# Gate and up of a SwiGLU feed-forward by seven products of block sums instead of eight, in three token blocks, with the last attention head reordered and merged in two halves

## The chip, the cores and the metric

One Trainium2 chip; the kernel runs on one core of it. Its engines are TensorE (PE in the profile; PEld is its weight load), VectorE (DVE), ScalarE (ACT), GpSimd (POOL) and SyncE (SP, which here issues the DMAs). The metric is the device time of one launch in microseconds; a kernel's time is the median of several runs.

## The reference

One layer for a prompt of 2048 tokens and a sample group of 8 x 4 tokens, all in float32, D = 1024, FF = 2816:

```python
z = rmsnorm(x, norm1_g) @ w_in                     # -> q, k, v (8 heads of 64), u, vg (8 groups of 64)
att = merge(three dilated sliding-window branches) # weights: each branch's share of the softmax sums
gate = spatial_gate(layernorm(vg)) 
x = x + concat([att, u * gate]) @ w_out
h = rmsnorm(x, norm2_g)
x = x + (silu(h @ w_gate) * (h @ w_up)) @ w_down
y = rmsnorm(x, final_g)
```

It returns y of both groups, the last keys and values of both, and the normalised v rows of the sample.

## The kernel before

Every operand of a matmul is a pair of float32r tiles, a high part and the low rest (`split_sb`, L120 to L126: the high part is a cast by ACT or DVE, the low part a subtraction, on POOL unless said otherwise), and every product is three matmuls: hi·hi, hi·lo, lo·hi. The engines' orders are written out by hand. In the attention part each piece of work is put at a step and a phase (`at(step, phase, fn)`), and a plan runs them in that order; in the feed-forward part `later(n, fn)` puts a piece n ticks ahead, and `tick()` runs what is due. Each engine works through its own queue in the order of issue and waits where an operand isn't ready.

The attention heads come one after another, 20 items each (16 band blocks, 4 strided groups "s"), in the order FIRST or OTHER. When a head's items are done, its softmax sums are brought into one layout (`stats_a` to `stats_c`, L959 to L974), turned into branch weights (`weights_a`, `weights_b`), written to a DRAM buffer f_d (`weights_store`) and read back in four chunks of 512 tokens (`merge_load`), by which the branches' outputs are multiplied and added (`merge`, L1008 to L1017, three steps per chunk) and stored (`merge_store`). For the last head this happens beside the start of the output projection: one chunk on DVE, three on POOL.

After that the tokens are worked through in two blocks, Block(0, 8) with 8 tiles of 128 tokens, and Block(8, 16), 8 tiles and the sample's 32 rows. In each: output projection (`out_part`, L1277 to L1279, k-tiles loaded by `load_cat`, split by `split_cat`, two halves of 512 columns), residual addition (`out_end`), RMSNorm (`norm2_a` to `norm2_c`; ACT squares, DVE multiplies by the factor and the gain, PE transposes, ACT and DVE split), then the feed-forward over 22 tiles f of 128 hidden columns:

- `load_gate` and `load_down` fetch 512 KB each for gate, up and down of one f; `split_gate` makes high and low parts of 128x1024 (ACT, POOL), `split_down` the same (DVE, POOL).
- `gate_unit` (L1336): for each slice of tokens (512 wide in block 1, 352 in block 2) 8 k-tiles for gate and 8 for up, three matmuls each (L1346 to L1348), into a PSUM tile of two banks, of which there are two; then ACT's silu (L1350), DVE's multiplication (L1351), high part on DVE (L125), low part on POOL (L126).
- `down_unit` (L1357): after each pair of f, for each token tile and each half of 512 columns, two f times three matmuls (L1372), and DVE's addition to the residual (L1374). PSUM has two banks for it.

At the end of a block come the final norm (`final_a`, `final_b`, L1377 to L1397: by DVE in one instruction, or for the first five tiles of the last block by ACT and POOL) and the store. Pieces of the caches (`roll`) are copied from DRAM to DRAM beside it.

## Time and profile before

| | |
|---|---|
| median of 3 runs | 2746.23 us (2745.55 to 2747.11) |
| the profiled execution | 2748.68 us, its span 2746.9 us |
| mean granted TensorE clock | 0.981 |
| instructions | 33610 |
| matmuls, gate and up / down | 3 x 1760 / 2112 |
| DMA | 367.44 MB, 134 GB/s over the span |

The page of the profile gives each engine's busy time with its share of the span, the granted clock and the DMA's share in slices, the chain of work that ended last (followed back from the last instruction, at each step to what released it), and the costliest groups: line, engine, operation, output<-inputs, shape, count | busy time, mean ns of one | idle time of the engine ahead of them and what ended it. The views used beside it are the groups with shapes kept apart, the busy time by stretch of the span, the chain in order of time, and the timeline (start, length, engine, line, operation, shape, count, in brackets the idle time before and its releaser).

### The profile page before, as it was taken

Reading aid. Unit: us, or ns where it says so; the run is one execution under the profiler, and the core shown is the slowest. Engines: PE = TensorE matmul, PEld = TensorE weight load, DVE = VectorE, ACT = ScalarE, POOL = GpSimd, SP = SyncE. Lnnn points to the kernel's source line nnn. Section 1 sums busy time; section 2 is a strip of 40 time slices with the busy share of each in tenths; the row PEclk is TensorE's granted clock in tenths of the full one; section 3 lists DMA queues with packets and bytes.
Section 4 is the critical chain, followed back from the end, with each engine's and each line's share of the span. In section 5 each row is a group of like instructions: output and inputs, shape, how many; then the busy total and the mean of one; then the engine's idle time right before and its main releaser. Section 6 shows DMA issues by size and latency. Waiting matters only on the chain.

```text
span 2746.9 us, 33610 instructions
## 1 busy us (share of the span) xinstructions
PE 2637.4 (96%) x13058; PEld 2234.2 (81%) x13058; DVE 1190.0 (43%) x2274; ACT 772.9 (28%) x1456; POOL 853.4 (31%) x561
## 2 busy tenths in 40 slices
PE   8998899998999989999999999999999999999997
PEld 6776777778888868888888888878899999999996
DVE  3268784436888755222222222264333232233225
ACT  6423344446777733100000001032200000000003
POOL 1035743231544542322222222211232222222222
PEclk9999999998999999999999999999999999999999
DMA  8664844685667473322222222272132222222211
GB/s 247 215 199 150 279 140 139 197 269 177 206 189 231 120 214 105 133 92 92 92 92 92 92 92 92 84 235 93 67 121 92 86 83 82 86 78 92 92 47 64
DMA packets 285476, 367.44 MB, mean 134 GB/s; under 512 B 18535, under 2 KB 214296, under 8 KB 279300
## 3 DMA queue, kind: packets, MB, share of 16 engines
q1 hardware_dynamic: 270948, 342.61, 38.2%
q10 hardware_dynamic: 14368, 22.68, 3.2%
q8 instruction: 103, 1.69, 0.3%
q14 instruction: 57, 0.47, 0.1%
HBM read 309.88 MB, written 125.47 MB: 158 GB/s over the span
## 4 chain that ended last, share of the span: by engine, by line
PE 61%; DVE 2%; DMA 1%; ACT 1%; SPq 0%; issue 0%; POOL 0%; ACTq 0%; DVEq 0%
PE ps_o L1372 18%; PE ps_s L1346 12%; PE ps_s L1347 12%; PE ps_s L1348 12%; PE ps_o L1279 2%; PE ps_o L1277 2%; PE ps_o L1278 2%; PE ps_t L1330 1%; DVE s L132 0%; DVE acc L1396 0%; DMA xl<-cat_d 0%; DMA acc<-in_x_prompt_dram 0%; DMA raw<-f_d 0%; DVE acc L1374 0%; SPq L1260 0%
## 5 line engine op out<-in xcount | busy, mean ns | idle before, releaser
L1346 PE MATMUL ps_s<-xh,gh 128*128 128x352 f32 (+1 forms) x1760 | 624.8, 355 | 0.0
L1348 PE MATMUL ps_s<-xh,gl 128*128 128x352 f32 (+1 forms) x1760 | 621.2, 353 | 0.0
L1347 PE MATMUL ps_s<-xl,gh 128*128 128x352 f32 (+1 forms) x1760 | 620.4, 352 | 0.0
L1372 PE MATMUL ps_o<-dw,hw 128*128 128x512 f32 x2112 | 500.0, 397 | 8.5 <-DVE acc L1374 8.5
L1372 PEld LDWEIGHTS ps_o<-dw,hw 128*128 128x128 f32 x2112 | 396.6, 189 | 107.0 <-DVE acc L1374 14.1
L1350 ACT ACTIVATE zn<-ps_s 128x352 f32<-128x352 f32 (+1 forms) x110 | 57.0, 518 | 1319.1 <-PE ps_s L1348 1319.1
L1351 DVE TENSOR_TENSOR zn<-zn,ps_s 128x352 f32<-128x352 f32 (+1 forms) x110 | 64.7, 588 | 722.8 <-ACT zn L1350 722.8
L1346 PEld LDWEIGHTS ps_s<-xh,gh 128*128 128x128 f32 x1760 | 332.6, 189 | 33.2
L1347 PEld LDWEIGHTS ps_s<-xl,gh 128*128 128x128 f32 x1760 | 331.8, 189 | 31.3
L1348 PEld LDWEIGHTS ps_s<-xh,gl 128*128 128x128 f32 x1760 | 330.8, 188 | 32.0
L1374 DVE TENSOR_TENSOR acc<-acc,ps_o 128x512 f32<-128x512 f32 x352 | 241.1, 687 | 214.5 <-PE ps_o L1372 214.5
L126 POOL TENSOR_TENSOR hw<-zn,hw 128x512 fp32r<-128x512 f32 (+2 forms) x110 | 119.6, 1087 | 662.4 <-DVE hw L125 648.8
L126 POOL TENSOR_TENSOR gl<-fr,gh 128x1024 fp32r<-128x1024 f32 x88 | 211.6, 2426 | 130.4 <-ACT gh L123 130.4
L126 POOL TENSOR_TENSOR dw<-fr,dw 128x1024 fp32r<-128x1024 f32 x44 | 106.6, 2422 | 377.6 <-DVE dw L125 377.6
L304 PE MATMUL ps_s<-wh,xh 128*128 128x512 f32 x480 | 198.9, 414 | 5.6 <-ACT xh L123 5.6
L305 PE MATMUL ps_s<-wl,xh 128*128 128x512 f32 x480 | 192.0, 400 | 1.2 <-DVE wl L212 1.2
L306 PE MATMUL ps_s<-wh,xl 128*128 128x512 f32 x480 | 191.8, 400 | 0.0
L304 PEld LDWEIGHTS ps_s<-wh,xh 128*128 128x128 f32 x480 | 93.3, 194 | 35.3 <-issue 8.4
L306 PEld LDWEIGHTS ps_s<-wh,xl 128*128 128x128 f32 x480 | 92.7, 193 | 20.8 <-DVE xl L126 0.2
L305 PEld LDWEIGHTS ps_s<-wl,xh 128*128 128x128 f32 x480 | 93.6, 195 | 19.3 <-DVE wl L212 2.1
L851 DVE CUSTOM_DVE_ANT_0 e<-ps_s,b 128x640 f32<-128x640 f32 (+4 forms) x128 | 93.7, 732 | 8.1 <-PE ps_s L845 8.1
L856 ACT ACTIVATE e<-e,st 128x640 f32<-128x640 f32 (+4 forms) x128 | 96.2, 751 | 0.8 <-DVE st L851 0.5
(368 smaller groups left out, 4012.2 us busy)
## 6 DMA issues: line engine op xcount, KB each, us to landing
out_ks_dram<-in_cache_k_dram SPq DMA_DIRECT2D x56, 512.0 KB
out_vs_dram<-in_cache_v_dram SPq DMA_DIRECT2D x56, 512.0 KB
fr<-in_w_gate_dram SPq DMA_DIRECT2D x44, 512.0 KB
fr<-in_w_up_dram SPq DMA_DIRECT2D x44, 512.0 KB
fr<-in_w_down_dram SPq DMA_DIRECT2D x44, 512.0 KB
raw<-in_w_in_dram SPq DMA_DIRECT2D x72, 256.0 KB
qk_d<-pair SPq DMA_DIRECT2D x64, 256.0 KB
pair<-f_d ACTq DMA_DIRECT2D x26, 512.0 KB
```

Of the source, the lines that this page charges most:

```text
L126: (eng_lo or pool).tensor_sub(lo, src, hi.bitcast(F32))
L304: pe.matmul(o[j], xh[:, k, :], wh, start=(k == 0), stop=False)
L305: pe.matmul(o[j], xh[:, k, :], wl, start=False, stop=False)
L306: pe.matmul(o[j], xl[:, k, :], wh, start=False, stop=(k == KD - 1))
L851: dve.tensor_tensor_reduce(e[:, 0:w], s[:, c0:c0 + w], d["b12"][:, 640 - w:640], 1.0, BIG, OP.add, OP.min, st[:, 0, n:n + 1])
L856: act.activation(e[:, 0:w], e[:, 0:w], AF.Exp, bias=st[:, 0, n:n + 1], scale=-1.0, accum_out=st[:, 1, n:n + 1])
L1346: pe.matmul(ps[:, q_, 0:n], wh[:, ks], B.xh[:, k, a:b], start=(k == 0), stop=False)
L1347: pe.matmul(ps[:, q_, 0:n], wh[:, ks], B.xl[:, k, a:b], start=False, stop=False)
L1348: pe.matmul(ps[:, q_, 0:n], wl[:, ks], B.xh[:, k, a:b], start=False, stop=(k == KD - 1))
L1351: dve.tensor_mul(sg[:, 0:n], sg[:, 0:n], ps[:, 1, 0:n])
L1372: pe.matmul(ps[0:nr], l_, r_[:, cs], start=(z == 0 and y == 0), stop=(z == FC - 1 and y == len(ops) - 1))
L1374: dve.tensor_add(B.acc[i][0:nr, cs], B.acc[i][0:nr, cs], ps[0:nr])
```

## The change

**Gate and up.** For a tile of 128 tokens and one f the two products gate and up are one product of a 2x2 block matrix (tokens in halves of 64; the 1024 inputs in halves of 512; columns gate and up). Winograd's form of Strassen's scheme computes it from seven block products instead of eight, with sums of blocks on both sides. The seven token operands are made once in a block, in `norm2_c`; the four sums of weight blocks and the seven splits for each f (`sums_a`, `sums_b`, `operand`); `product` runs the seven products of an f and combines them on the way. Each product has 4 k-tiles x 3 matmuls, 64 columns for each tile of the block (and 4 sample columns for each tile of the last block).

**Blocks.** Three: tiles 0 to 5, 6 to 11, and 12 to 15 with the sample; a matmul is 384, 384 and 272 columns wide. f = 0 runs in two units (tiles 0 to 3 and 4, 5; in the last block two and two). The downs of a pair of f run inside the next even f, after products 2 to 5; those of the last pair at the start of the next block. Weights are fetched once for each block.

**Engines.** In `norm2_b` and `final_b` ACT multiplies by the factor and POOL by the gain, where DVE did both (in `final_b` for all tiles of the first two blocks). The high part of the down weights comes from ACT, the low part from POOL for an even f and from DVE for an odd one. The low part of the operands of products 3 and 6 of the next f comes from DVE where f is even, all others from POOL.

**Last head.** Its items come in the order LAST; its first half of rows is brought to weights inside the head (steps 14 to 16), chunks 0 and 1 are merged there, one on DVE and one on POOL, and stored; chunks 2 and 3 follow in `first_block`. Of the head before it, the last chunk and store come later. `Stats` holds the functions of before with a range of rows.

```diff
+    class Stats:
+        def __init__(self, h, st, r0=0, r1=P):
...
+        def store(self):
+            n = self.r1 - self.r0
+            act.dma_start(dap(f_d, self.h * 2 * T + self.r0 * NT, [[NT, n], [T, 2], [1, NT]]), self.f[self.r0:self.r1, 0:2, :])
...
+    LAST = [0, "s", 1, "s", 2, "s", 3, "s", 4, 5, 6, 7] + list(range(8, NT))
...
+            stats_of(h, [(x + y, ph) for y, ph in ((14, "early"), (14, "turn"), (15, "early"), (15, "misc"), (16, "early"), (16, "mid"))], 0, 64)
+            at(x + 18, "mid", merge_load, h, 0)
+            at(x + 18, "mid", merge_load, h, 1)
+            for part in range(3):
+                at(x + 20 + part, "store", merge, h, 0, dve, part)
+                at(x + 20 + part, "store", merge, h, 1, pool, part)
+            at(x + 23, "store", merge_store, h, 0, 2)
...
+    TOK = (0, 4, 1, 3, 5, 2, 6)
...
     def fraw():
-        return pool_["fw"].tile([P, 1024], F32, name="fr", tag="fr", bufs=2)
+        return pool_["fw"].tile([P, 512], F32, name="fr", tag="fr", bufs=6)
+    def op_tile():
+        t_ = pool_["fg"].tile([P, 2, 512], F32R, name="op", tag="op", bufs=8)
+        return t_[:, 0], t_[:, 1]
...
     def norm2_b(B, i, xn, s1):
-        dve.scalar_tensor_tensor(xn[:n], B.acc[i][:n], r, gain[0][:n], op0=OP.mult, op1=OP.mult)
+        act.activation(xn[:n], B.acc[i][:n], AF.Copy, scale=r)
+        pool.tensor_mul(xn[:n], xn[:n], gain[0][:n])
...
+        def sums_of():
+            act.activation(t4, b12, AF.Copy)
+            dve.tensor_sub(t1, t4, b11)
+            dve.tensor_sub(t3, b22, t4)
+            dve.tensor_sub(t2, b22, t1)
+            dve.tensor_sub(t4, b21, t2)
...
+            for s_, j in zip(sums, (3, 5)):
+                split_sb(at_(hi, j, j + 2), at_(lo_, j, j + 2), s_)
...
+    def sums_a(f):
+        a11, a21, a22, a12 = (ab.pop((f, q)) for q in range(4))
+        s3, s2 = (raw_tile(), raw_tile()) if f == 0 else (lambda t_: (t_[:, 0], t_[:, 1]))(pair_tile(F32))
+        dve.tensor_sub(s3, a11, a21)
+        dve.tensor_add(a21, a21, a22)
+        dve.tensor_sub(s2, a21, a11)
+        ab[f] = [a11, s2, a12, a21, s3, s2, a22]
+    def sums_b(f):
+        dve.tensor_sub(ab[f][5], ab[f][2], ab[f][1])
+    def operand(f, q, eng_lo=None):
+        ops[f, q] = op_tile()
+        split_sb(*ops[f, q], ab[f][q], eng_lo=eng_lo)
...
+    def split_down(f, eng_lo=None):
+        wd[f % FC] = ob_pair("dw")
+        split_sb(*wd[f % FC], raws.pop(("d", f)), eng_lo=eng_lo)
+    def product(B, u, q):
...
+        if q % 2 == 0:
+            u["s"] = ps_s() if q < 6 else ps_t()
...
+        for k in range(4):
+            ks = slice(k * P, (k + 1) * P)
+            pe.matmul(out, wh[:, ks], xh[:, :, k], start=(k == 0), stop=False)
+            pe.matmul(out, wh[:, ks], xl[:, :, k], start=False, stop=False)
+            pe.matmul(out, wl[:, ks], xh[:, :, k], start=False, stop=(k == 3))
...
+        if q == 0:
+            act.activation(c11, ps, AF.Copy)
+        elif q == 1:
+            dve.tensor_add(c12, c11, ps)
+        elif q == 2:
+            dve.tensor_add(c11, c11, ps)
+            act.activation(c11, c11, AF.Silu)
+        elif q == 3:
+            act.activation(c22, ps, AF.Copy)
+        elif q == 4:
+            dve.tensor_add(c21, c12, ps)
+            pool.tensor_add(c12, c12, c22)
+            pool.tensor_add(c22, c22, c21)
+        elif q == 5:
+            dve.tensor_add(c12, c12, ps)
+            act.activation(c12, c12, AF.Silu)
+        elif q == 6:
+            dve.tensor_add(c21, c21, ps)
+            dve.tensor_mul(c12, c12, c22)
+            dve.tensor_mul(c11, c11, c21)
...
+                split_sb(hi, lo_, g[:, :, 0:64], eng_hi=dve)
...
-        if i < B.nt - 3 and B.last:
+        if i < B.nt - 3 or not B.last:
             act.activation(x, x, AF.Copy, scale=r)
             pool.tensor_mul(x, x, gain[1][:n])
...
-    blocks = [Block(0, 8), Block(8, NT)]
+    blocks = [Block(0, 6), Block(6, 12), Block(12, NT)]
...
+            if f + 1 < NF:
+                if q == 0:
+                    sums_a(f + 1)
+                operand(f + 1, q, dve if f % 2 == 0 and q in (3, 6) else None)
+                if q == 3:
+                    sums_b(f + 1)
+            loads_ = {0: (0, 1), 2: (2,), 4: (3,)}.get(q, ())
+            if f + 2 < NF:
+                quarters(f + 2, *loads_)
...
+            if f % 2 == 0 and q == 6:
+                split_down(f)
+                load_down(f + 1)
+            elif f % 2 == 1 and q == 3:
+                split_down(f, eng_lo=dve)
...
+            for q in range(7):
+                one(u, q)
+                if u["f"] % 2 == 0 and u["f"] > 0 and 2 <= q < 6:
+                    downs_of((B.h[0], B.h[1]), *((0, 1), (1, 2), (2, 4), (4, 9))[q - 2])
...
-    nc = _bacc.Bacc("TRN2", target_bir_lowering=False, num_devices=1)
+    nc = _bacc.Bacc("TRN2", target_bir_lowering=False, num_devices=1, dynamic_dma_scratch_size=1024)
```

The prediction names lines of the changed kernel: L1411 to L1413 are the three sums in `sums_a`, L1447 to L1449 the matmuls in `product`, L1457 the addition at q = 1 there.

More of the change, by code (lines that the diff above doesn't have):

```diff
@@ L1062, in hymba_step @@
         r4 = 0
[L1063 removed]
+        for n in FIRST if h == 0 else LAST if h == H - 1 else OTHER:
             if n == "s":
@@ new lines, in next_block @@
+    def next_block(B, downs):
+        n = len(B.rows)
+        order = [n - 1] * B.last + list(range(B.nt))
+        B.banks = (tuple(order[0:2]), tuple(order[2:4]), tuple(order[4:6]))
+        B.place()
+        tiles = [i for i in order if B.rows[i] == P]
+        for i in tiles[:2]:
+            load_cat(B, i, 0, KD)
+        skip = n - len(tiles)
+        for j, i in enumerate(tiles):
+            if j > 1:
+                later(2 * j - 1, load_cat, B, i, 0, KD)
+            later(4 + 2 * (j + skip), split_cat, B, i)
+        later(1, half1_load, 0, 1, 2, 3, 4, 5)
+        k = len(downs) + 1
+        for y, i in enumerate(order):
+            later(k + 2 * y + 5, open_end, B, i)
+        for y, what in enumerate(([(half1_split, B, 0, 1)], [(half1_split, B, 2, 3), (half1_load, 6, 7)],
+                                  [(half1_split, B, 4, 5), (quarters, 0, 0, 1)], [(half1_split, B, 6, 7), (quarters, 0, 2, 3)],
+                                  [], [(quarters, 1, 0, 1)])):
+            later(k + y, both, *what)
+        for fn in downs:
+            fn()
+        for i in order:
+            open_unit(B, i)
+        first_operands(1)
+        for i in order:
+            second_end(B, i, second_unit(B, i))
+        if B.last:
+            norm2_c(B, n - 1, B.xns)
```

570 lines of the change are left out of this document (294 added, 276 removed).

## The prediction

> **What bounds the kernel now.** I read the page first: the share of each engine, then the chain that ended last by engine, then the costliest groups.
>
> ```profile
> span 2746.9 us, 33610 instructions
> PE 2637.4 (96%) x13058; PEld 2234.2 (81%) x13058; DVE 1190.0 (43%) x2274; ACT 772.9 (28%) x1456; POOL 853.4 (31%) x561
> PE 61%; DVE 2%; DMA 1%; ACT 1%; SPq 0%; issue 0%; POOL 0%; ACTq 0%; DVEq 0%
> L1346 PE MATMUL ps_s<-xh,gh 128*128 128x352 f32 (+1 forms) x1760 | 624.8, 355 | 0.0
> L1372 PE MATMUL ps_o<-dw,hw 128*128 128x512 f32 x2112 | 500.0, 397 | 8.5 <-DVE acc L1374 8.5
> ```
>
> TensorE is busy 96% of the span, and the last chain is its own work; the gate/up products (three lines like L1346) and the downs (L1372) stand idle for 0.0 and 8.5 us. An average over stages doesn't tell where the idle rest lies, so next come the busy times by stretch: the change of stage from attention to the output projection, block 1's FFN, the change of block, block 2's projection end, block 2's FFN, the tail. Columns: stretch, its length, then PE, PEld, DVE, ACT, POOL busy with counts, granted clock, DMA share, GB/s.
>
> ```profile
> 965.00:1030.00 65.00, 52.58 (x221) 40.70 (x221) 32.89 (x49) 20.03 (x37) 25.07 (x16) 0.92 0.75 225
> 1100.00:1813.00 713.00, 713.00 (x3058) 574.18 (x3056) 181.89 (x279) 69.65 (x92) 206.27 (x106) 1.00 0.28 96
> 1813.00:1834.00 21.00, 16.82 (x62) 11.95 (x60) 18.82 (x45) 8.20 (x19) 0.00 (x0) 0.92 1.09 317
> 1936.00:1951.00 15.00, 9.97 (x58) 8.82 (x56) 11.03 (x25) 8.41 (x16) 2.82 (x1) 0.89 0.00 0
> 1951.00:2702.00 751.00, 751.00 (x4172) 698.48 (x4173) 212.56 (x355) 69.97 (x108) 215.14 (x150) 1.00 0.25 84
> 2702.00:2747.00 45.00, 26.27 (x110) 19.17 (x108) 32.55 (x71) 19.42 (x35) 13.05 (x7) 0.89 0.25 97
> ```
>
> In both FFN stretches PE is busy all the time at clock 1.00: there a matmul removed is time removed, until another engine becomes late. POOL works 206.3 + 215.1 = 421 us there, DVE 394. The idle of the four other stretches is 12.4 + 4.2 + 5.0 + 18.7 = 40.3 us.
>
> **What the change takes from TensorE.** Busy times of matmuls overlap, so the price of one is the distance between starts. I take 512 wide from one step of the chain of waits, the others from the timeline.
>
> ```profile
> 1133.09 22.39 PE ps_o L1372 x96
> 2088.12 0.32 PE L1348 MATMUL ps_s<-xh,gl 128*128 128x352 f32 x1
> ...
> 2094.95 0.33 PE L1348 MATMUL ps_s<-xh,gl 128*128 128x352 f32 x1
> 916.29 0.34 PE L896 MATMUL ps_o<-ph,ve 128*128 128x384 f32 x1
> 916.47 0.33 PE L896 MATMUL ps_o<-pl,ve 128*128 128x384 f32 x1
> 916.64 0.28 PE L896 MATMUL ps_o<-ph,ve 128*128 128x256 f32 x1
> 916.76 0.28 PE L896 MATMUL ps_o<-pl,ve 128*128 128x256 f32 x1
> 907.57 0.27 PE L945 MATMUL ps_o<-el,v 128*128 128x128 f32 x1
> ...
> 908.24 0.28 PE L945 MATMUL ps_o<-el,v 128*128 128x128 f32 x1
> ```
>
> 512 wide: 22.39 / 96 = .233 us. 352: the two quoted starts are 42 matmuls apart, 6.83 / 42 = .163. 384: .17 to .18; 256: .12; 128: 6 steps, .67 / 6 = .112. The line through 512 and 352 (.44 ns a column) puts 384 at .176, which fits, and 272, which no row shows, at .127. From below it is bounded by the 256 row (.12), from above by the 352 row (.163); I take .127, next to the 256 row.
>
> Before, the 22 gate/up tiles f cost 22 × 48 × 2 = 2112 matmuls of 512 in block 1 and 22 × 48 × 3 = 3168 of 352 in block 2: 492.5 + 515.1 = 1007.6 us. After, each f has 7 products × 4 k-tiles × 3 = 84 matmuls, 384 wide in blocks 1 and 2, 272 wide in block 3, and f = 0 runs as two units. Blocks 1 and 2: 21 × 84 × .176 + 84 × .12 (256) + 84 × .112 (128) = 330 each; block 3: 1764 × .1273 + 168 × .112 = 243.4. Sum 903.4: **104 us less**. Downs, transposes and output projection keep their number.
>
> **What it adds beside TensorE.** Per f seven operands of 128x512 are made where two of 128x1024 were, after four sums of weights on DVE; the weights are read for three blocks instead of two; the combining of products is two ACT copies, five DVE additions and two POOL additions on top of what was there. The prices:
>
> ```profile
> L126 POOL TENSOR_TENSOR dw<-fr,dw 128x1024 fp32r<-128x1024 f32 x22 | 52.7, 2395 | 201.0 <-DVE dw L125 201.0
> L126 POOL TENSOR_TENSOR hw<-zn,hw 128x352 fp32r<-128x352 f32 x44 | 41.5, 942 | 191.0 <-DVE hw L125 191.0
> L1351 DVE TENSOR_TENSOR zn<-zn,ps_s 128x352 f32<-128x352 f32 x65 | 33.8, 521 | 354.8 <-ACT zn L1350 354.8
> L125 DVE CAST hw<-zn 128x320 fp32r<-128x320 f32 x21 | 6.9, 327 | 0.7
> 311.04 1.28 POOL L521 TENSOR_TENSOR pr<-kv,qb 96x512 f32<-96x512 f32 x1
> 311.31 4.05 DVE L212 SCALAR_TENSOR_TENSOR wl<-raw,g1c,wh 128x512 fp32r<-128x512 f32 x1 [2.53 <-ACT wh L206]
> ...
> 313.53 1.28 POOL L521 TENSOR_TENSOR pr<-kn,qb 128x512 f32<-128x512 f32 x1
> 996.86 1.77 DVE L1268 TENSOR_TENSOR xl<-xl,xh 128x512 fp32r<-128x512 f32 x1
> 998.04 1.74 POOL L1015 TENSOR_TENSOR o<-o,zn 128x512 f32<-128x512 f32 x1
> 998.55 1.64 DVE L1268 TENSOR_TENSOR xl<-acc,xh 128x384 fp32r<-128x384 f32 x1
> 1001.69 0.68 DVE L1268 TENSOR_TENSOR xl<-xl,xh 128x512 fp32r<-128x512 f32 x1
> 1002.36 0.56 DVE L1268 TENSOR_TENSOR xl<-acc,xh 128x384 fp32r<-128x384 f32 x1
> ```
>
> POOL takes 2.40 for 128x1024, 1.28 for 128x512, and by the 352 row about 1.03 for 384. An odd f costs it seven operands (9.0), two low parts of the hidden values (2.0) and two additions (2.0): 13.0 us beside 84 × .176 = 14.8 of PE; an even f has five operands and a down (6.4 + 2.4 + 4.0 = 12.8), and PE has the downs as well. So POOL's total (about 846 us against 421) isn't a bound. But the last rows show that a DVE instruction with two SBUF sources and a POOL instruction don't run together: one 128x512 subtraction on DVE takes .68 alone and 4.05 while POOL's instructions (the first and the last of three quoted) run beside it; at 996 to 1000 us they alternate (DVE starts at 996.86 and 998.55, POOL between them at 998.04), a pair in 1.6 to 1.7, which is POOL's 1.28 and some .4 for DVE.
>
> The place where this reaches PE follows from the order of the changed program. PE's products 4 and 5 of a unit use the PSUM tile of products 0 and 1, which is free when DVE has added product 1 (L1457). On DVE's queue, ahead of that addition in an odd f, stand: the end of the f before (addition, two multiplications, two casts: .56 + .56 + .56 + .36 + .36 = 2.4), the low part of operand 6, and the three weight sums (L1411 to L1413). All four of these last have two SBUF sources, and POOL at that time has ready: two low parts of hidden values, the 2.40 of an even down, the first operand: 1.03 + 1.03 + 2.40 + 1.28 = 5.7 us. If they alternate as at 996 us, the addition is done at 2.4 + 5.7 + 4 × .4 + .3 (rest of the last sum) + .56 = 10.6 after the end of the unit before; PE is there at 4 × 12 × .176 = 8.45. **PE waits 2.1 us in each of 20 odd units of blocks 1 and 2: 42 us.** In an even f the down is off POOL (5.7 − 2.4), the subtraction is off DVE, and downs stand between PE's products: no wait. In block 3 PE is there at 4 × 12 × .127 = 6.1, DVE (narrower) at 10.2: 4.1; and the downs in the next even f, due after product 2 (4.6), find the low hidden part about 2.4 late in the same alternation: **6.5 × 10 = 65**. From below this is zero (rival 1). From above, each of the four instructions waits for everything ready on POOL, as at 311 us; POOL's 5.7 can't pass twice, so this changes the order, not the sum. I take the alternation: the row at 996 us has the same shapes.
>
> The Trainium skill ("SBUF — State Buffer", section "SBUF: two separate sides") says that a GpSimd instruction, or a DVE one with two SBUF inputs, takes the shared port pair for its whole length and blocks the other. The blocking agrees with the 4.05; the length does not quite, since whole lengths would make a pair 1.28 + .68 = 1.96, and the rows show 1.6 to 1.7. By the page each of the four would cost .68 rather than .4, 1.1 us more in 30 units, and the result would be some 33 us higher.
>
> **Transitions.** There are now two changes of block and three ends of projection. The chain to the first product goes through ACT and POOL for the gain and seven token operands per tile. The final norm's POOL multiplication now serves all tiles of blocks 1 and 2; in the tail that gives:
>
> ```profile
> 2725.42 3.07 PE L1372 MATMUL ps_o<-dw,hw 128*128 128x512 f32 x12 [0.21 <-DVE acc L1374]
> 2726.03 2.40 POOL L1394 TENSOR_TENSOR acc<-acc,final_g 128x1024 f32<-128x1024 f32 x1 [1.72 <-ACT acc L1393]
> ...
> 2726.27 2.18 DVE L132 SCALAR_TENSOR_TENSOR s<-s 128x1 f32<-128x1 f32 x1
> ...
> 2729.55 3.06 PE L1372 MATMUL ps_o<-dw,hw 128*128 128x512 f32 x12 [1.06 <-DVE acc L1374]
> 985.03 7.51 DMA raw<-f_d
> 985.97 0.80 PE L1277 MATMUL ps_s<-gh,xh 128*128 128x512 f32 x1 [4.75 <-ACT xh L1267]
> ...
> 992.04 0.60 PE L1278 MATMUL ps_s<-gl,xh 128*128 128x512 f32 x1
> 992.47 0.40 PE L1279 MATMUL ps_s<-gh,xl 128*128 128x512 f32 x1
> ```
>
> A tile's period is 4.13 instead of 12 × .233 = 2.8 us: the norm's 128x1 step on DVE lasts as long as POOL's multiplication beside it, and the additions that free PSUM stand behind it. For two block changes I take 5 each (the row of the one: 4.2), for three projection ends 6 each (one now: 5.0, longer chain), for the start 10 (now 12.4, half of the merge is gone from it), for the tail 15 (now 18.7; the block is half as long): 53 against 40.3, **+13**. Bounds: no change, and double the increase (0 to +26).
>
> The last head's order and half merge: the load of f_d took 7.51 us, and the merge of chunks 0 and 1 now follows it inside the head, where DVE may wait some 2.5 us in its order and PE, with work of other items queued, may not. 0, bounds −4 and +4. The weights' third reading: DMA share was .28 and .25 in the FFN; per f the same bytes come in three quarters of the time, at most .4. No cost; if a quarter came late, PE would wait at product 0.
>
> **The sum.** 2748.7 (profiled execution: span 2746.9 and 1.8 around it) − 104 + 42 + 65 + 13 + 0 = 2764.7. The median of the runs, 2746.23, is 2.5 lower: **2762**.
>
> **Rivals.**
> *Rival 1: the alternation doesn't reach PE, faster.* Should the sums get in ahead of POOL's 2.40 (the down's high part comes from ACT, behind operand 6's, so it may be ready late), DVE is done at 10.6 − 2.4 = 8.2, ahead of PE, and only block 3 waits, about 2 × 10 = 20. 2762 − 107 + 20 = 2675; 2655 to 2700. For it: DVE is idle over half the time. Against it: the alternation at 996 us needs only that both have work.
> *Rival 2: the waits cost clock, slower still.* After 4.75 idle the quoted matmuls start .43 apart until 992.5, then .233: 14 of them lose about 3 us. If block 3's 4.1 us waits each do that, + 30: 2792; if blocks 1 and 2's waits grow to 4 as well, 2815 and more. It decides at some length of the wait up to that 4.75; against it speaks that block 3's 4.1 is shorter.
> The Trainium skill ("TensorE: Matmul & The Clock Gate", section "Part 1: The HAM clock gate") has the clock halved after a stretch without activity of a few us; the row at 985.97 agrees.
> That the change doesn't remove what it says is excluded: the changed program's order has the 84 matmuls.
>
> **How the numbers follow.** The forecast's case, 2735 to 2790, .48 (.02 of it faster, .08 within 0.2%, .38 slower); rival 1 .33; rival 2 .15; something better than all of these, below 2655, .04. 0.2% (2740.7 to 2751.7) is about what a measurement of this kernel can tell from no change. Faster .02 + .33 + .04 = .39, same .08, slower .38 + .15 = .53. The range 2668 to 2818 leaves out the lower third of rival 1, the rest below it and the top of rival 2, some .2. The slower cases' own range is 2752 to 2790.
>
> **What would show it.** Product lines with starts .176 and .127 apart; the three sums' mean well over .68 (1.3 to 1.7); in odd f a PE wait at product 4 released by the addition L1457, 2.1 us in blocks 1 and 2, 4.1 in block 3; a pair of f in 48.5 us (46.4 without waits), block 3 40.7 (34.2); POOL near 55% in the FFN; clock under 1.00 in block 3 for rival 2. If the sums' mean stays near .7 and L1457 releases nothing, step and forecast are wrong and rival 1 holds.

## The result, and the profile after

The changed kernel takes 3052.47 us (median of 4 runs, 3047.75 to 3056.89) where the kernel before takes 2745.89 in the same comparison: a ratio of 1.112 (95% interval 1.109 to 1.114). The forecast was 2762, its range ended at 2818. The profiled execution took 3056.9 us, 308 more than that of before.

The page of the changed kernel, in the lines that answer to those shown of before:

```profile
span 3055.1 us, 38250 instructions
PE 2674.5 (88%) x13578; PEld 2321.2 (76%) x13578; DVE 1768.3 (58%) x3073; ACT 1134.8 (37%) x2175; POOL 1487.6 (49%) x1138
PE 51%; DVE 15%; ACT 5%; issue 4%; POOL 4%; DMA 3%; SPq 1%; ACTq 0%; DVEq 0%; POOLq 0%
L1500 PE MATMUL ps_o<-dw,hw 128*128 128x512 f32 x2112 | 516.2, 397 | 12.1 <-DVE acc L1502 4.7
```

TensorE is busy 88% instead of 96%, and the last chain goes through DVE, ACT, POOL and the DMA for a quarter of the span, where it had been TensorE's own work. The groups by line say where TensorE stands idle; the numbers behind the last bar are the idle time and the three releasers that ended most of it.

```profile
L1447 PE MATMUL ps_s<-xh,op 128*128 128x384 f32 (+4 forms) x1656 | 574.3, 347 | 199.9 <-DVE zn L1464 88.1 <-DVE raw L1459 64.1 <-ACT raw L1455 20.1
L1365 PE MATMUL ps_t<-ident,pair 128*128 128x128 f32 x128 | 23.6, 344 | 48.2 <-POOL pair L1350 43.4 <-DVE xl L1384 4.8
```

Two hundred microseconds ahead of the products, and none of the three releasers is L1457, the addition that the forecast had named. Ahead of the norm's transposes 48 us, where before it was 5.0:

```profile
L1330 PE MATMUL ps_t<-ident,pair 128*128 128x128 f32 (+1 forms) x136 | 19.0, 281 | 5.0 <-DVE xl L1334 5.0
```

The busy times by stretch (end of the first projection, the feed-forward of blocks 1, 2 and 3) have the clock in the column after the five engines:

```profile
1083.00:1115.00 32.00, 22.47 (x141) 21.00 (x141) 16.97 (x40) 12.96 (x24) 16.09 (x12) 0.81 0.00 1
1115.00:1700.00 585.00, 522.04 (x2558) 473.54 (x2558) 326.28 (x435) 149.39 (x266) 313.13 (x233) 0.96 0.34 115
1840.00:2440.00 600.00, 536.02 (x2614) 484.94 (x2614) 337.91 (x456) 156.45 (x278) 316.51 (x235) 0.96 0.34 113
2548.00:3025.00 477.00, 403.65 (x2402) 364.53 (x2402) 258.22 (x453) 136.93 (x257) 294.88 (x268) 0.91 0.22 67
```

Before, both feed-forward stretches had every microsecond busy at 1.00. Now a share of 11% to 15% is idle, and the clock is below 1.00 as well.

**One odd f.** The timeline of PE in block 1, only the matmuls that waited, and DVE and POOL beside it:

```profile
1345.42 0.44 PE L1447 MATMUL ps_s<-xh,op 128*128 128x384 f32 x1 [0.64 <-ACT raw L1455]
1352.20 0.44 PE L1447 MATMUL ps_s<-xh,op 128*128 128x384 f32 x1 [2.28 <-DVE raw L1459]
1358.61 0.44 PE L1447 MATMUL ps_s<-xh,op 128*128 128x384 f32 x1 [1.91 <-DVE zn L1464]
```

```profile
1342.76 0.56 DVE L1471 TENSOR_TENSOR raw<-raw,ps_t 128x384 f32<-128x384 f32 x1 [1.49 <-PE ps_t L1449]
...
1344.66 3.02 POOL L126 TENSOR_TENSOR hw<-zn,hw 128x384 fp32r<-128x384 f32 x2 [6.59 <-DVE hw L125]
1344.71 0.68 DVE L126 TENSOR_TENSOR op<-fr,op 128x512 fp32r<-128x512 f32 x1
1345.31 1.50 DVE L1411 TENSOR_TENSOR pair<-fr 128x512 f32<-128x512 f32 x1
1346.85 1.39 DVE L1412 TENSOR_TENSOR fr<-fr 128x512 f32<-128x512 f32 x1
1347.64 2.84 POOL L126 TENSOR_TENSOR dw<-fd,dw 128x1024 fp32r<-128x1024 f32 x1
1348.27 2.75 DVE L1413 TENSOR_TENSOR pair<-fr 128x512 f32<-128x512 f32 x1
1350.95 0.54 DVE L1457 TENSOR_TENSOR raw<-raw,ps_s 128x384 f32<-128x384 f32 x1
1351.59 0.55 DVE L1459 TENSOR_TENSOR raw<-raw,ps_s 128x384 f32<-128x384 f32 x1
```

The unit starts at 1342.50. Product 1 should follow product 0 at 1344.6 and starts at 1345.42, as soon as ACT has copied product 0. Product 2 runs at once. Product 3 should start at 1349.8 and starts at 1352.20, when DVE has added product 2. Product 5 waits for the addition of product 4. Each pair of products writes the two banks of one PSUM tile, and **the second of a pair starts only when the result of the first has been read**. DVE's lateness is what the forecast had described: three sums of .68 us take 1.50, 1.39 and 2.75, the last one as long as POOL's 2.84 beside it, ending .54 after it. (The Trainium skill, "SBUF — State Buffer", section "SBUF: two separate sides", has the other engine blocked for the whole instruction; this row nearly agrees, since .54 is less than the .68 of a subtraction alone.) But the price is paid at product 3, where PE has 2.1 us of slack less, and every product 1 waits for ACT's copy.

In block 3 the wait at product 5 is longer. The chain of waits, in order of time:

```profile
2702.36 2.89 POOL dw L126
2705.27 3.60 DMA fd<-in_w_down_dram
2708.89 1.07 ACT dw L123
2709.98 1.74 DVE dw L126
2711.72 0.36 DVE zn L1464
2712.12 0.60 PE ps_s L1447
2712.72 0.23 PE ps_s L1448
...
2716.57 0.19 PE ps_t L1447
2716.77 0.13 PE ps_t L1448
```

POOL's low part of the even down frees the one buffer `fd`; then come the load of the odd down, its two parts, and only then, on DVE, the addition of product 4. And after the wait the matmuls stand .23 apart instead of .13 for 4.6 us: the clock has halved.

**The account.** I added up the distances between the starts of all matmuls, from the first product to the last. At steps close to the prediction's (.1755 for 384 columns, .1265 for 272, .120 for 256, .112 below) the products take 900.0 us; 322 us more lie between their starts: some 223 us of waits and 99 us of slow matmuls. (The waits are the 199.9 us of idle time of the row above. The profile counts idle time from the end of the last matmul, which comes some .16 us later than its step, and there are about 140 waits.) Against before that is −108 + 322. The norm's transposes wait 43 us more. What is left of the 308, some 50 us, lies in the output projections, the rest of the norms and the last head.

### The profile page after: what moved, and what is told of

The parts are those of the page before. It is cut to its first block, busy times and chain, and to the rows that moved or that the text cites. A ratio compares the mean times of both kernels' runs of the same rounds, so it can differ in the third digit from the quotient of the medians.

```text
span 3055.1 us, 38250 instructions
## 1 busy us (share of the span) xinstructions
PE 2674.5 (88%) x13578; PEld 2321.2 (76%) x13578; DVE 1768.3 (58%) x3073; ACT 1134.8 (37%) x2175; POOL 1487.6 (49%) x1138
## 4 chain that ended last, share of the span: by engine, by line
PE 51%; DVE 15%; ACT 5%; issue 4%; POOL 4%; DMA 3%; SPq 1%; ACTq 0%; DVEq 0%; POOLq 0%
PE ps_o L1500 16%; PE ps_s L1447 7%; PE ps_s L1449 6%; PE ps_s L1448 6%; DVE dw L126 2%; DVE pl L882 2%; PE ps_t L1447 2%; PE ps_t L1449 2%; PE ps_t L1448 1%; DVE fr L1412 1%; PE ps_o L896 1%; DMA fd<-in_w_down_dram 1%; PE ps_s L845 1%; POOL dw L126 1%; ACT dw L123 1%
## 5 line engine op out<-in xcount | busy, mean ns | idle before, releaser
L1447 PE MATMUL ps_s<-xh,op 128*128 128x384 f32 (+4 forms) x1656 | 574.3, 347 | 199.9 <-DVE zn L1464 88.1
L1448 PE MATMUL ps_s<-xl,op 128*128 128x384 f32 (+4 forms) x1656 | 557.4, 337 | 0.0
L1449 PE MATMUL ps_s<-xh,op 128*128 128x384 f32 (+4 forms) x1656 | 555.6, 335 | 0.0
L1500 PE MATMUL ps_o<-dw,hw 128*128 128x512 f32 x2112 | 516.2, 397 | 12.1 <-DVE acc L1502 4.7
L1447 PEld LDWEIGHTS ps_s<-xh,op 128*128 128x128 f32 x1656 | 339.0, 205 | 243.5 <-DVE zn L1464 98.2
L1502 DVE TENSOR_TENSOR acc<-acc,ps_o 128x512 f32<-128x512 f32 (+1 forms) x374 | 254.2, 687 | 216.3 <-PE ps_o L1500 216.3
L126 POOL TENSOR_TENSOR op<-fr,op 128x512 fp32r<-128x512 f32 x214 | 311.6, 1465 | 93.9 <-ACT op L123 93.9
L126 POOL TENSOR_TENSOR op<-pair,op 128x512 fp32r<-128x512 f32 x189 | 243.5, 1289 | 216.6 <-ACT op L123 216.6
L1448 PEld LDWEIGHTS ps_s<-xl,op 128*128 128x128 f32 x1656 | 340.0, 205 | 4.3
L1449 PEld LDWEIGHTS ps_s<-xh,op 128*128 128x128 f32 x1656 | 339.2, 205 | 0.0
L123 ACT ACTIVATE op<-pair 128x512 fp32r<-128x512 f32 x189 | 117.6, 622 | 244.0 <-DVE pair L1413 217.7
L123 ACT ACTIVATE op<-fr 128x512 fp32r<-128x512 f32 x280 | 173.0, 619 | 14.5 <-PE ps_s L1312 12.7
L126 POOL TENSOR_TENSOR hw<-zn,hw 128x384 fp32r<-128x384 f32 (+2 forms) x66 | 78.5, 1202 | 154.9 <-DVE hw L125 133.5
L306 PEld LDWEIGHTS ps_s<-wh,xl 128*128 128x128 f32 x480 | 91.8, 191 | 20.8 <-POOL xl L126 0.3
```

The costliest lines, as they stand in the source:

```text
L123: act.activation(hi, src, AF.Copy)
L126: (eng_lo or pool).tensor_sub(lo, src, hi.bitcast(F32))
L306: pe.matmul(o[j], xl[:, k, :], wh, start=False, stop=(k == KD - 1))
L1447: pe.matmul(out, wh[:, ks], xh[:, :, k], start=(k == 0), stop=False)
L1448: pe.matmul(out, wh[:, ks], xl[:, :, k], start=False, stop=False)
L1449: pe.matmul(out, wl[:, ks], xh[:, :, k], start=False, stop=(k == 3))
```

## The experiments

Times are medians; the ratio is that to the kernel before, measured on the same chip, with its interval. The chips differ: the kernel before took 2745.89 us beside the changed kernel and 2748.24 to 2750.73 beside the experiments, so a difference between two chips is good to some 5 us.

### Single-bank tiles: e1

```diff
-        if q % 2 == 0:
-            u["s"] = ps_s() if q < 6 else ps_t()
-        ps = u["s"][:, q % 2, 0:n] if q < 6 else u["s"][:, 0:n]
+        ps = (ps_q() if q < 6 else ps_t())[:, 0:n]
...
```

`ps_q` gives tiles of [128, 512], one bank, with four buffers, in a pool of its own (`reuse_waits="tile"`). The output projections of blocks 2 and 3 take one of these tiles where they took a tile of two banks.

> Products 0 to 5 write four PSUM tiles of one bank each instead of two tiles of two banks; nothing else differs. Tie theory (the second product of a two-bank tile can only start when the first one's result has been read, so products 1, 3 and 5 wait for the copy L1455 and the additions L1459 and L1464): these waits vanish, with them 223 us of waits and most of the 98 us of slow matmuls behind them; 3052 - 290 = 2760, 2735 to 2790, and the first blocks' pair of f takes 46 to 47 us. Port theory (the prediction's: DVE is late since it shares a port with POOL, and any product that needs DVE will wait): the waits move to later products, and the time stays above 2950.

Measured: 2908.66 us, 1.057 (1.054 to 1.059): 144 us less than the changed kernel, half of what the tie theory expected, and less than the port theory allowed.

```profile
L1450 PE MATMUL ps_q<-xh,op 128*128 128x384 f32 (+4 forms) x1656 | 542.3, 327 | 13.7 <-DVE zn L1467 9.1 <-ACT xh L128 4.3 <-DVE raw L1460 0.3
L1503 PE MATMUL ps_o<-dw,hw 128*128 128x512 f32 x2112 | 557.7, 415 | 94.1 <-DVE hw L130 45.4 <-POOL hw L131 44.0 <-DVE acc L1505 4.7
```

The waits ahead of the products go from 199.9 to 13.7 us, so the tie is shown. Each product had a bank to itself before as well; what differs is the tile, and the pool, that the banks belong to. With four tiles the place of product 1 is next needed by product 5 and not by product 4, so the edit loosens the wait that the forecast had named as well. But the downs now wait 94.1 instead of 12.1, for the high and the low part of the hidden values: DVE and POOL are as late as before, and PE meets them at the next place that needs them. Each theory is half right, and neither range was met.

### The sums left out: e2 and e3

```diff
-        dve.tensor_sub(s3, a11, a21)
-        dve.tensor_add(a21, a21, a22)
-        dve.tensor_sub(s2, a21, a11)
+        act.activation(s3, a11, AF.Copy)
+        act.activation(a21, a22, AF.Copy)
+        act.activation(s2, a21, AF.Copy)
```

These versions leave the three sums out, so they don't compute the layer; they serve to price the sums.

> The three weight sums L1411 to L1413 are replaced by three copies on ACT, so that the sums are left out; DVE has one instruction with two SBUF sources ahead of its first additions in an odd f instead of four. Port theory: waits and slow clock in odd f go, 2900 or less. Tie theory: product 1 goes on waiting 0.8 us for the copy in every f, product 3's wait falls from 2.6 to 0.8, product 5's stays at 1.8 (4.7 in the last block), since it hangs on another DVE instruction: 3052 - 21 x (1.8 + 1.0) = 2990, 2970 to 3020.

Measured: 2982.22 us, 1.084 (1.082 to 1.087), 70 us less, in the tie theory's range. The waits for L1459 fall from 64.1 to 20.1 us, those for the copies stay at 20.1 (and 19.6 under the tile's other name), those for L1464 stay near 88.1, at 84.8. What is left at product 3 is .6 us of idle time each, as much as at product 1.

> Both edits: single-bank tiles, and the weight sums left out (ACT copies instead). Tie theory: with four banks DVE's lateness of some 3 us is hidden already, so this is within 20 us of the single banks alone. Port theory: it is 100 us or more below them.

Measured: 2824.03 us, 1.027 (1.025 to 1.029). That is 85 us below e1, not within 20 (nor 100 or more, as the port theory had it): **the tie theory's claim that four banks hide DVE's lateness falls.** The sums cost 70 us with tied banks and 85 without. The two causes add up: 144 + 85 of the 308 us. In blocks 1 and 2 of e3 a pair of f takes 46.4 us, which the prediction had for no wait; in block 3 it takes 39.0, where 34.2 would be no wait. Leaving the sums out takes away DVE's own work on them (.68 us each when alone) together with the turns with POOL; these runs don't separate the two.

### The norm's order: e4, and both: e6

```diff
-            later(2, norm2_c, B, i, xn)
+            due[clock[0] + 2, 10 ** 9 + len(seq)] = (norm2_c, (B, i, xn))
+            seq.append(0)
```

The large number puts `norm2_c` last in its tick.

> At one tick the scaling of the next tile (norm2_b) is issued ahead of the token operands of the tile before (norm2_c), which in the changed kernel stand first on DVE. Chain theory (PE's 48 us ahead of the transposes L1365 are a loop: transposes, DVE's seven subtractions, the next tile's Newton steps, ACT, POOL's gain multiplication, next transposes): the idle time ahead of L1365 falls below 15 us and the time to 3022, 3010 to 3035. Rival (POOL's multiplication of 2.35 us is late by itself, whatever stands ahead on DVE): 3045 to 3056.

Measured: 3019.58 us, 1.098 (1.096 to 1.100): 33 us less, in the chain theory's range, though the idle time falls to 18.6 us and not below 15.

```profile
L1366 PE MATMUL ps_t<-ident,pair 128*128 128x128 f32 x128 | 20.4, 304 | 18.6 <-DVE xl L1385 12.3 <-POOL pair L1350 6.3
```

The idle time ahead of the transposes falls from 48.2 to 18.6, and POOL's share of it from 43.4 to 6.3: the 2.35 us of POOL's multiplication weren't too long, they started too late, because the Newton steps of the next tile stood on DVE behind the subtractions of the tile before.

> Single-bank tiles and the norm's order together. The two waits lie in different stages, so the gains add: 2909 - 33 = 2876, 2865 to 2887. Rival (the time that the norm's order gives is lost again in the feed-forward, which then starts with less work done ahead): 2895 or more.

Measured: 2862.48 us, 1.042 (1.039 to 1.044). 46 us less than e1, just below the range; the gains add, with some more.

### Downs later, down weights elsewhere: e7, e9, e8

```diff
-                if u["f"] % 2 == 0 and u["f"] > 0 and 2 <= q < 6:
-                    downs_of((B.h[0], B.h[1]), *((0, 1), (1, 2), (2, 4), (4, 9))[q - 2])
+                if u["f"] % 2 == 0 and u["f"] > 0 and 3 <= q < 6:
+                    downs_of((B.h[0], B.h[1]), *((0, 1), (1, 3), (3, 9))[q - 3])
```

> As e6, and the downs of a pair run after products 3 to 5 of the next even f instead of 2 to 5. Hidden theory (with single banks the wait has moved to the downs, 124 us ahead of L1503, since the high and low parts of the odd f's hidden values aren't ready after product 2): one product more hides 2.1 us in the first two blocks, 1.5 in the last, 21 + 11 times: the waits ahead of the downs fall to 65 or less and the time to 2815, 2795 to 2835. Rival (DVE and POOL together are the bound, since they share a port): the wait moves to the products, 2860 or more.

Measured: 2947.04 us, 1.072 (1.070 to 1.073): 85 us slower than e6, where it should have been 61 below the 2876 that were expected of e6. The waits for the hidden values fell as expected, from 87.5 to 43.4 us, but a new one of 95.3 us came:

```profile
L1504 PE MATMUL ps_o<-dw,hw 128*128 128x512 f32 x2112 | 583.4, 434 | 139.6 <-DVE acc L1506 95.3 <-DVE hw L130 24.0 <-POOL hw L131 19.4
```

```profile
1348.65 1.05 DVE L131 TENSOR_TENSOR op<-fr,op 128x512 fp32r<-128x512 f32 x1 [2.00 <-ACT op L128]
1349.62 0.68 DVE L1424 TENSOR_TENSOR pair<-fr,pair 128x512 f32<-128x512 f32 x1
1350.23 1.27 DVE L1506 TENSOR_TENSOR acc<-acc,ps_o 128x512 f32<-128x512 f32 x2
...
1350.95 1.65 PE L1504 MATMUL ps_o<-dw,hw 128*128 128x512 f32 x3 [3.00 <-DVE acc L1506]
```

After product 3 the operand's low part and the fourth sum are issued to DVE first. DVE stands idle for 2.00 us until ACT has the high part, and the two additions that free the downs' banks stand behind it, with nothing to hinder them but the order.

```diff
-            elif f % 2 == 1 and q == 3:
+            elif f % 2 == 1 and q == 5:
                 split_down(f, eng_lo=dve)
```

> As e6, and in an odd f the down weights are split after product 5 instead of after product 3. Buffer theory (the odd down's low part on DVE waits for a chain: POOL's low part of the even down frees the one buffer, its load of 3.6 us, ACT's high part; and DVE's additions of products 4 and 5 and all of the hidden values stand behind it): in the last block the hidden values come some 3 us earlier, 11 times, in the first two about 0.5: 2876 - 45 = 2831, 2815 to 2850. Rival (the port's total): 2865 or more.

Measured: 2872.49 us, 1.045 (1.043 to 1.047), no gain over e6: a miss. The waits of products fall from 16.5 to 8.0, those of the downs rise from 91.8 to 104.9. The down's low part no longer holds up the addition of product 4, but now, on DVE for some 2 us, the addition and the multiplications of product 6.

> As e7 with the split after product 5 as well. If both waits hang on their places, they add: 2780, 2760 to 2805, and the last block's pair falls from some 40 to 36 us. Rival (the port's total of DVE and POOL is the bound in the last block): within 15 us of e7.

Measured: 2944.29 us, 1.070 (1.068 to 1.073), the same as e7, as the rival had it, though for e7's reason.

### Downs ahead of the operand: e10, e11, e12

```diff
             if u["b"] < B.nt:
                 return
+            if f % 2 == 0 and f > 0 and 3 <= q < 6:
+                downs_of((B.h[0], B.h[1]), *((0, 1), (1, 3), (3, 9))[q - 3])
...
-                if u["f"] % 2 == 0 and u["f"] > 0 and 2 <= q < 6:
-                    downs_of((B.h[0], B.h[1]), *((0, 1), (1, 2), (2, 4), (4, 9))[q - 2])
```

> As e7 (downs after products 3 to 5), but each group of downs is issued ahead of that product's operand work and not behind it. Queue theory (in e7 DVE's additions L1506, which free the downs' two PSUM banks, stood in DVE's order behind the operand's low part and the fourth sum, which come late: 95 us of waits): these waits go and the hidden values' 43 us stay, against 119 in e6: 2862 - 70 = 2792, 2775 to 2815. Rival (the port's total of DVE and POOL binds): 2850 or more.

Measured: 2832.31 us, 1.031 (1.028 to 1.033): 115 below e7, 30 below e6. The waits for L1506 fall from 95.3 to 28.0, so the order was the cause of most of them; the rest of the expected gain didn't come.

```profile
L1504 PE MATMUL ps_o<-dw,hw 128*128 128x512 f32 x2112 | 536.0, 405 | 71.5 <-DVE acc L1506 28.0 <-DVE hw L130 24.1 <-POOL hw L131 19.0
```

```diff
-            elif f % 2 == 1 and q == 3:
+            elif f % 2 == 1 and q == 6:
```

> As e10, and an odd f's down weights are split after product 6, behind the hidden values' high parts on DVE, instead of after product 3. Order theory (after product 3 the low part of the down holds up the additions of products 4 and 5, after product 5, as in e9, the multiplications; after product 6 nothing that PE needs soon): 20 to 30 us less than e10, 2765, 2745 to 2785. Rival (port total): within 10 us of e10.

Measured: 2830.49 us, 1.029 (1.027 to 1.031), the same as e10: the rival. The low part of the down can be put at three places (after product 5 in e9) and costs about the same at each.

> As e11 with the three weight sums left out (copies on ACT in their place). Order theory: DVE's lateness is hidden by then, so at most 15 us less than e11. Port theory (what DVE and POOL do in turns is still the bound of the last block): 30 us or more less than e11, nearly all of it in the last block.

Measured: 2755.94 us, 1.002 (1.001 to 1.003), 75 us less than e11. That is more than the order theory's 15: DVE's lateness is not hidden. But the port theory had nearly all of it in the last block, and it isn't there: from the first product of f = 1 to the last of f = 21, blocks 1, 2 and 3 take 479, 479 and 386 us, where e11 takes 501, 499 and 417. So removing the sums still pays in every block, after every change of order, and only block 3 still waits then: a pair of f takes 46.4 us in blocks 1 and 2, the prediction's figure for no wait, and 37.4 in block 3, where that is 34.2. As in e3, the turns at the port aren't separated from DVE's own work.

### The operands read back: e13

```diff
+            if again[0]:
+                sync.dma_start(both_, op_d[f * 7 + q])
+                return
             split_sb(*ops[f, q], ab[f][q], eng_lo=eng_lo)
+            later(3, sync.dma_start, op_d[f * 7 + q], both_)
```

`again[0]` is set for the second and third block; `both_` is the operand's tile, high and low part together. The quarters and the sums are skipped in those blocks.

> As e10, and the seven split operands of each f are written to DRAM as they are made in the first block; the second and third block read them back (one transfer of 512 KB each) instead of loading, adding and splitting the weights again. That takes the sums, the seven casts and all seven low parts off DVE, ACT and POOL in two of three blocks; 81 MB more are written, 161 MB more read, 104 MB of quarters not loaded. Port theory (what is left of the waits in e10, 83 us ahead of the downs, 21 ahead of products, 26 of slow clock, comes from DVE and POOL taking turns): nearly all of it goes in blocks 2 and 3, some 95 us: 2832 - 95 = 2737, 2715 to 2765. Rival (the transfers come late, or slow others down): PE waits for op_d, 2800 or more.

Measured: 2759.45 us, 1.003 (1.002 to 1.005): 73 us less than e10. The stretches of blocks 2 and 3 of e13:

```profile
1810.00:2250.00 440.00, 429.78 (x2206) 396.61 (x2206) 167.71 (x288) 61.90 (x101) 107.14 (x93) 1.00 0.62 241
2380.00:2700.00 320.00, 315.31 (x2027) 284.88 (x2026) 143.74 (x298) 48.17 (x92) 81.50 (x118) 0.99 0.62 239
```

and of e10:

```profile
1810.00:2250.00 440.00, 427.51 (x2170) 390.61 (x2169) 304.69 (x374) 122.89 (x223) 268.93 (x195) 0.99 0.39 129
2450.00:2750.00 300.00, 266.42 (x1668) 235.06 (x1667) 204.57 (x312) 94.61 (x180) 213.73 (x185) 0.98 0.28 81
```

In block 3 of e10 DVE and POOL are busy for 418 us of 300 together, and PE 89% of the time; in e13 they are busy for 225 us of 320, and PE 99%. The 418 count an instruction that is held up by the other engine as busy. An estimate without that takes, for each shape, the shortest duration in this trace: POOL's work in the 300 us of e10 is then 181 us, DVE's with two SBUF sources 71, and the rest of DVE's 90. Neither engine would be full by itself; POOL's and DVE's two-source work in strict turns would take 252 of the 300. A pair of f there takes 34.8 us (median) between the starts of its downs, 40.7 in e10, 44.3 in the changed kernel; the prediction had 34.2 for no wait. Reading back costs little: PE waits 7.7 us in all for op_d, at 240 GB/s.

```profile
L1468 PE MATMUL ps_q<-xh,op 128*128 128x384 f32 (+4 forms) x1656 | 532.3, 321 | 13.4 <-DMA op<-op_d 7.7 <-ACT xh L131 1.8 <-DVE zn L1485 1.6
```

Block 1, which makes and writes the operands, doesn't gain: from f = 1 to f = 21 it takes 508 us, and 491 in e10. Block 3 takes 363 instead of 421.

### What is left: b1, e14, e15, e16

The kernel before, with one edit:

```diff
+    LAST = [0, "s", 1, "s", 2, "s", 3, "s", 4, 5, 6, 7] + list(range(8, NT))
...
-        for n in OTHER if h else FIRST:
+        for n in FIRST if h == 0 else LAST if h == H - 1 else OTHER:
```

> The kernel before, with the last head's items in the order LAST and nothing else. Order theory (the output projection starts 11 us later in the changed kernel because the strided items come early and leave a last stretch of bands that waits for DVE): 10 us slower than before. Rival (it is the half sums and the merge that now stand among the items on DVE and POOL): within 4 us of before.

Measured: 2759.41 us, 1.0035 (1.0023 to 1.0047), against 2750.73: 9 us, the order theory's. It has neither the half sums nor the early merge, and the output projection starts as late as in the changed kernel (980.1 and 980.2 us, 968.7 before). Its stretch from 900 to 940 us, and that of before:

```profile
900.00:940.00 40.00, 37.40 (x209) 35.23 (x208) 27.90 (x68) 23.64 (x57) 18.84 (x16) 0.83 0.26 55
```

```profile
900.00:940.00 40.00, 38.52 (x246) 35.23 (x246) 32.24 (x82) 30.46 (x73) 17.81 (x15) 0.96 0.41 104
```

In this stretch the clock is .83 against .96, which the busy share hides (37.4 against 38.5); the matmuls done say it better, 209 against 246. In the next 40 us it is the other way round, .96 against .91. From 850 to 980 us PE is busy for 114.9 us against 119.4, so waits have a part in it too; how the 9 us divide isn't settled.

```diff
-                if q == 3:
+                if q == 4:
                     sums_b(f + 1)
```

> As e13, with the fourth weight sum issued after product 4 instead of after product 3. Theory (in the first block the downs' additions L1523 wait 20 us, since the fourth sum, ahead of them on DVE, overwrites a tile that POOL's low part of operand 1 has yet to read): the 20 us go, 2759 - 17 = 2742, 2735 to 2750, the first version under the kernel before. Rival (the additions wait for the operand's low part on DVE, which comes late by itself): 2752 or more.

Measured: 2753.45 us, 1.0012 (0.9998 to 1.0025): 6 us less than e13, a third of what was expected; the waits for the downs' additions L1523 fall from 21.7 to 14.9, not to zero. It can't be told from the kernel before.

```diff
+        if B.last:
+            units = [dict(f=f, a=0, b=B.nt) for f in range(NF)]
+            for _ in range(4):
+                tick()
```

> As e14, with f = 0 of the last block in one unit of 272 columns instead of two of 136. The two halves take 168 matmuls of .112 us, and in the changed kernel all of them ran at half the clock, some 34 us; one unit takes 84 of .127, 11 us, but starts only when the last tile's norm is through, some 10 us later. Theory (slow short matmuls cost more than the cover they give): 10 us less than e14. Rival (the cover is worth as much): within 4 us of e14 or above.

Measured: 2755.57 us, 1.002 (1.001 to 1.003): no gain over e14; the cover is worth about what the slow matmuls cost.

```diff
-    LAST = [0, "s", 1, "s", 2, "s", 3, "s", 4, 5, 6, 7] + list(range(8, NT))
+    LAST = [0, 1, "s", 2, "s", 3, 4, "s", 5, "s", 6, 7] + list(range(8, NT))
```

(with the half sums and the first merge two steps later)

> As e14, with the strided items of the last head spread over its first ten places instead of the first eight, and its half sums and first merge two steps later. Order theory (b1_last: the crowded strided items alone cost 9 us, by waits for DVE in that stretch and the clock of .83 behind them): 4 to 8 us less than e14, 2747, 2742 to 2750, at or just under the kernel before. Rival (any early place of the strided items costs as much, or the later merge is waited for at the output projection): 2752 or more.

Measured: 2751.99 us, 1.0005 (0.9995 to 1.0015): 1.5 us less than e14, between the two theories, inconclusive. It stands level with the kernel before. No version tried is faster than it.

## Why the prediction was wrong

**The matmuls that the change removes** were counted and priced rightly: 903.4 us forecast, 900.0 at the steps measured between waits. The removed time is there; three times as much was lost again.

**The step that failed** is "PE's products 4 and 5 of a unit use the PSUM tile of products 0 and 1, which is free when DVE has added product 1". It followed the tile from one pair of products to the next and left out the pair itself: the second product of a tile waits for the reader of the first. So PE had no slack of two pairs (8.45 us) to set against DVE's 10.6, but none at all at products 1, 3 and 5, and no product 4 waits in any f. Single banks (e1) take 186 of the 200 us of these waits away and 144 us of the time. "In an even f: no wait" failed with it: product 1 waits in every f. A pair of f takes 54.8 us in blocks 1 and 2, where 48.5 were forecast, and 44.3 in block 3, where it was 40.7.

**DVE's lateness** was real, and smaller than forecast. The sums were forecast at 1.3 to 1.7 us, and in block 1 they take 1.47, 1.63 and 1.94 on the mean, as the turns with POOL would have it. But in block 3, where the forecast had its larger term, they come near the .68 of one alone:

```profile
L1413 DVE TENSOR_TENSOR pair<-fr 128x512 f32<-128x512 f32 x21 | 19.0, 906 | 0.7
L1412 DVE TENSOR_TENSOR fr<-fr 128x512 f32<-128x512 f32 x21 | 18.7, 891 | 0.7
L1411 DVE TENSOR_TENSOR pair<-fr 128x512 f32<-128x512 f32 x21 | 14.5, 691 | 0.0
```

In the odd f with sums beside them, the addition L1457 ends 9.3 us after the start of the unit on the mean of blocks 1 and 2, where 10.6 were forecast, and 6.0 us in block 3, where 10.2 were, just ahead of PE's 6.1. So by the forecast's own wait PE would have lost about 1 us in blocks 1 and 2 and not 2.1, and at product 4 in block 3 nothing instead of 4.1. (One of the rows behind the forecast was also misread: the 4.05 us are those of a multiplication and subtraction in one, which takes .74 as a rule.) e2, e3 and e12 show that leaving the sums out is worth 70 to 85 us, whatever the banks. Rival 1, that the lateness doesn't reach PE, is refuted. What was missing is that its place isn't product 4 alone: take one wait away and the next consumer of DVE and POOL pays (the downs in e1, the additions in e7, those of product 6 in e9), until in e12 and e13 the work itself goes.

**In block 3** 6.5 us a pair were forecast. The wait at product 5 alone is 4.6 on the mean (50.2 us in 11), and it comes from a chain that the forecast did not have, through the one buffer of the down weights. That the idle time of a pair, 6.6 us in all, comes near the 6.5 is luck. Moving the down's low part (e9, e11) gains nothing; this suggests that other chains are nearly as long, which no run shows by itself.

**Rival 2**, waits that cost clock, was priced at 30 us and a chance of .15, as a case of its own. It isn't a rival but a second price on the first: 99 us of slow matmuls beside 223 us of waits, 68 of them in odd f, where the long waits are, and 26 in f = 0. In e1, where the waits are gone, the clock of blocks 1 and 2 is back (.99 from 1115 to 1600 us, 1.00 from 1850 to 2250, .96 in both before that edit).

**The transitions** were forecast at +13. The norm's transposes alone wait 43 us more: the step "the chain to the first product goes through ACT and POOL" named the engines and priced each end at 6 us by the 5.0 of before, without the order on DVE that makes a loop of them (e4: 33 us come back with one line moved).

**The last head** was forecast at 0 with −4 to +4; the order of its items alone costs 9 us (b1), and the merge shows no price beside it. Why the spread-out order of e16 gains little isn't settled, and a version with the last head as it was isn't tried.

**What keeps e16 level with the kernel before.** From start to start its matmuls of gate and up take 930 us, 83 less than before. The output projections lose 41 of this again, the downs 29, the norms' transposes 11 and the heads some 3. (The output projection starts 9 us later, but 8 matmuls of the heads, 5.9 us, that stood behind its start now stand ahead of it.) Why the projections lose so much isn't settled: no version keeps two blocks of tokens, so the price of the third isn't known.

## What to carry to other kernels

When two results share a PSUM tile, follow the wait within the tile as well as from tile to tile, in the program's order of waits: the second product of a pair had no slack at all. A reduction of matmuls pays only if the engines that prepare and combine have room in the stage where they run: add up POOL and DVE's instructions with two SBUF sources together, at their undisturbed lengths, and set that against TensorE's time after the reduction, not before it (in e10's last block an estimated 252 us in 300, and PE 89% busy). And moving an instruction in an in-order queue moves the wait to whatever stands behind it; only work that is removed, as the operands in e13 that are made once and read back, takes the wait away.

## What the runs showed of the hardware

How long TensorE may wait before its clock falls: I took each wait ahead of a product from f = 1 on (from the end of the last matmul's step to the next start) and what the product then took over its steps. After the 86 waits under 2 us it lost .1 us; of 22 between 2.0 and 2.5 us 8 were followed by slow matmuls; after all 21 longer ones the product lost .7 to 1.8 us. The waits come several to an f, so one wait isn't seen by itself. In the stretch from 2712 us shown above, after an idle time of 4.88 us, the clock is .50 for 4.6 us:

```profile
2712.00:2716.60 4.60, 4.48 (x20) 4.48 (x21) 0.51 (x2) 0.81 (x2) 2.75 (x3) 0.50 0.76 228
```

The Trainium skill ("TensorE: Matmul & The Clock Gate", section "Part 1: The HAM clock gate") gives a window of some 3.4 us without activity; here slow matmuls come after some waits from 2.0 us on. Also not expected: 161 MB read back beside everything else, at 240 GB/s, made PE wait under 8 us in e13. The 81 MB written fall in block 1, which was 17 us longer than in e10.
